# Where the merge of a hybrid decoder layer reads back the stored output of its linear attention

## The chip, the cores and the metric

The kernel runs on one core of a Trainium2 chip. Its time is the device time of one execution in microseconds (us). Five engines work side by side, each through its own instructions in order: TensorE (PE; its weight loads are listed as PEld), VectorE (DVE), ScalarE (ACT), GpSimd (POOL) and SyncE (SP), which here issues nearly all DMA transfers.

## What is computed

One layer over 1,088 tokens (1,024 of a prompt, 64 of eight samples), width 1,024. Two token mixers stand side by side: a sparse attention whose keys an indexer picks, and a gated linear attention ("GLA"). Both are projected, merged by gates, projected again, and followed by a norm, an MLP and another norm.

```python
attn = attend(q_a, k_a, v_a, q_i, k_i, z['w_i'])
...
o_b = (o_b.reshape(b, t, GLA_DV_TOT) * jax.nn.silu(z['g_b'].astype(jnp.float32))).astype(x.dtype)
branch_a = attn @ w_attn_o
branch_b = o_b @ w_gla_o
merged = jax.nn.sigmoid(z['gate_a']) * branch_a + jax.nn.sigmoid(z['gate_b']) * branch_b
return merged @ w_out, k_a, v_a, k_i, s_new.astype(x.dtype)
```

The change lies between `o_b`, `attn` and `branch_b`.

## The kernel before

**Tiling.** Activations are held feature-major: 8 pages of 128 features by 1,088 tokens, cut into token chunks of 384, 384 and 320 (`CH`, "c0", "c1", "c2" below). A product in 32-bit precision is made of three matmuls on a high and a low part of each operand (`mm3`, line 612): so each operand is split, its high part written by an ACT copy, its low part by a subtraction on DVE or POOL.

**Jobs.** `main` (line 1639) runs a list of jobs, one weight page of 128 columns each; PE's stream is made of them. Towards the end of the first phase stand the last gate jobs (PE rows `gate`), then from `merge_at` on eight jobs of branch B (`gated_job`, line 1526, PE rows `pmb`), then eight of branch A (`pma`), then the output projection (`pwo`). A job of branch B reads all eight pages of the GLA output: 24 matmuls for each of the three chunks, 72 in all. Its result is multiplied into a gate page (`mgt`) on DVE. A job's weights (`wr`) are split into `wh` (ACT) and `wl` (POOL or DVE) by `w_split`, one job ahead; `env["alone"]` makes the first job of branch B an exception, so that the second one's weights are split only after the first one's instructions.

**Other streams.** Around the jobs, generators run as streams: the prompt's softmax (`at_soft`: scores `psq`, exponentials, scaling of `pp`) and its products with the values (`at_pv`, line 1390: transposes `ppt`, split `phl`, sums `pov`), 32 units of a query tile and a head pair. Each unit ends in `tail` (line 1393): its output `ao` is split into `ahl` (two buffers, line 1402) and stored to `at_s` by two DMAs, from where branch A loads it later. The GLA output was stored to `ob_s` long before, in jobs `gb`; `ob_load` (line 1502) loads its eight pages `obl` in two pieces each (384 columns for c0, 704 for c1 and c2) and splits them into `obh` (ACT) and `obl` in place (`sub`).

**What sets the order.** All instructions are recorded in one pass by a planner: `Clock` keeps an estimated time for each engine and buffer, `Order.run` (line 297) steps the first stream of its list whose wish time is not after PE's estimated time. What is recorded first stands first in each engine's queue. `sub` (line 404) gives a subtraction to POOL when its estimate ends there before DVE's estimate plus `late`. All instructions are recorded through one line (254), so the profile shows that line throughout, and tiles tell the groups apart.

**DMA issue.** SP issues in order. By the built program each issue also waits until the eighth DMA before it has completed, so that at most eight are under way.

Of the kernel before, what the change touches and what calls it, by code (L numbers as in the profile page):

```python
# [12 lines left out]
F32 = mybir.dt.float32  # L13
F32R = mybir.dt.float32r
# [9 lines left out]
P = 128  # L24
# [30 lines left out]
LATE_I = 1.5  # L55
VAHEAD = 1
SCRATCH = 4096
OBLEAD = 3
NPV = 32
GAHEAD = 2  # L60
BLEAD = 1
DEEP = 2
# [20 lines left out]
def f32(ap):  # L83
    return ap.bitcast(F32)
# [288 lines left out]
def front(ph, tc, env, A, O):  # L373
# [13 lines left out]
    def page(name, dt=F32, shape=None):  # L387
        return clock.take(pgs.tile(shape or [P, T], dt, name=name, tag="pg", bufs=NPG), name, "pg", NPG)
# [4 lines left out]
        return clock.take(pgs.tile([p, n], dt, name=name, tag="sm", bufs=NSM), name, "sm", NSM)  # L393

    def tiny(name, n=8, dt=F32, p=P):
        return pgs.tile([p, n], dt, name=name, tag="ty", bufs=24)

    def cst(name, shape, dt=F32):
        return cs[0].tile(shape, dt, name=name, tag=name, bufs=1)

    def csg(name, shape, dt=F32):
        return gpool.tile(shape, dt, name=name, tag=name, bufs=1)

    def sub(out, a, b, late=0.0):

        n = out.free_size() if callable(out.free_size) else out.free_size
        if clock.t["pool"] + 0.0021 * n < clock.t["dve"] + 0.00104 * n + late:
            pool.tensor_tensor(out, a, b, op=OP.subtract)
        else:
            dve.tensor_sub(out, a, b)  # L410
# [897 lines left out]
    def loadq(i):  # L1308
        if i < len(units):
            qt, hp = units[i]  # L1310
            qs[i] = cs[0].tile([P, 2, P], F32R, name=f"qq{qt}{hp}", tag="qq", bufs=3)
            sp.dma_start(f32(qs[i]), f32(qa_s[2 * hp:2 * hp + 2, :, qt * P:(qt + 1) * P].rearrange("h p q -> p h q")))

    def kv_load(g):
# [75 lines left out]
    def at_pv():  # L1390
        tails = deque()

        def tail(qt, hp, po):

            yield [po]
            o = small("ao", 256)
            t = small("ao2", 256)
            act.activation(t[:64], po[64:128], AF.Copy)
            dve.tensor_tensor(o[:64], po[0:64], t[:64], op=OP.add)
            unpin(po)  # L1400
            yield [o[:64]]
            hl = cs[0].tile([P, 256], F32R, name="ahl", tag="ahl", bufs=2)
            act.activation(hl[0:64], o[:64], AF.Copy)
            sub(hl[64:128], o[:64], f32(hl[0:64]))
            yield [hl]
            c, x0 = qt // 3, (qt % 3) * P
            for e in range(2):
                sp.dma_start(view(f32(at_s[c]), 2 * hp * 64 * 768 + e * 384 + x0, [[768, 64], [64 * 768, 2], [1, P]]),
                             f32(hl[e * 64:e * 64 + 64].rearrange("p (h q) -> p h q", q=P)))

        def step():

            while tails and all(clock.ready(x) <= clock.t["pe"] + 0.3 for x in tails[0][1]):
                tails[0][1] = next(tails[0][0], None)
                if tails[0][1] is None:
                    tails.popleft()
        for _ in units:
            yield lambda: len(soft) > 0
            (qt, hp), pd = soft[0]
            vp = kv["v", hp // 2]  # L1420
            po = bank("pov", True)[:, :256]
            pend = deque()

            def flush(kt, m, hl, last):
                for j in range(m):
                    for e in range(2):
                        pe.matmul(po, vp[:, kt + j], hl[:, e, 256 * j:256 * j + 256],
                                  start=kt + j + e == 0, stop=last and j == m - 1 and e == 1)
            for kt in range(0, qt + 1, 2):
                yield pd  # L1430
                m = min(2, qt + 1 - kt)
                pt = bank("ppt")[:, :256 * m]
                for j in range(m):
                    for h in range(2):
                        pe.transpose(pt[:, (2 * j + h) * P:(2 * j + h + 1) * P], pd[h][:, (kt + j) * P:(kt + j + 1) * P], idf)
                hl = page("phl", F32R, [P, 2, 512])
                act.activation(hl[:, 0, :256 * m], pt, AF.Copy)
                dve.tensor_sub(hl[:, 1, :256 * m], pt, f32(hl[:, 0, :256 * m]))
                pend.append((kt, m, hl))
                step()  # L1440
                if len(pend) > 1:
                    yield [pend[0][2]]
                    flush(*pend.popleft(), False)
                    step()
            soft.popleft()
            while len(tails) > 1:
                yield tails[0][1]
                step()
            while pend:
                yield [pend[0][2]]  # L1450
                flush(*pend.popleft(), not pend)
            tails.append([tail(qt, hp, po), ()])
            kv["pv"] = kv.get("pv", 0) + 1
        while tails:
            yield tails[0][1]
            step()
# [42 lines left out]
    merge_at = len(jobs)  # L1499
    mark["search"] = merge_at + SEARCH  # L1500

    def ob_load():
        yield lambda: kv.get("pv", 0) >= NPV and state["job"] >= merge_at - OBLEAD or state["job"] >= merge_at
        raw = [page(f"obl{k}", F32R) for k in range(8)]
        for s in (slice(0, 384), slice(384, T)):
            for k in range(8):
                sp.dma_start(f32(raw[k][:, s]), ob_s[k][:, s])
        for c, (c0, n) in enumerate(CH):
            s = slice(c0, c0 + n)
            for k in range(8):  # L1510
                yield [f32(raw[k][:, s])]
                if c == 0:
                    ob.append((page(f"obh{k}", F32R), raw[k]))
                h, l = ob[k]
                act.activation(h[:, s], f32(l[:, s]), AF.Copy)
                sub(l[:, s], f32(l[:, s]), f32(h[:, s]))
            flags.add(("ob", c))

    gts = {}
# [147 lines left out]
    s_ts = order.add(top_sample(), slack=TS_SLACK, margin=M_TS)  # L1667
    s_main = order.add(main(), engines=())
    order.add(at_load(), at=0)
    order.add(ob_load(), slack=1.0, at=0)  # L1670
    s_pv = order.add(at_pv(), margin=M_PV, at=1)
    s_sf = order.add(at_soft(), margin=M_SF, at=2)
    env.update(ka_n=ka_n, v_n=v_n, ix_k=ix_k, ix_v=ix_v, p_b=p_b, p_q=p_q)
# [3 lines left out]
def back(ph, tc, env, A, O):  # L1677
# [9 lines left out]
    def page(name, dt=F32R):  # L1687
        return clock.take(pgs.tile([P, 2, 384], dt, name=name, tag="pg", bufs=NBP), name, "bpg", NBP)
# [7 lines left out]
        return clock.take(pgs.tile([P, 384], dt, name=name, tag="sm", bufs=NBS), name, "bsm", NBS)  # L1696

    def own(name, shape, dt=F32, bufs=1):
        return pgs.tile(shape, dt, name=name, tag=name, bufs=bufs)

    def sub(out, a, b):
        n = out.free_size() if callable(out.free_size) else out.free_size
# [89 lines left out]
    def ln(c, z, s, gi, emit, tag):  # L1792
        n = CH[c][1]
        last = z[7:] if c == 2 else []
        for k, x in enumerate([s] + last):
            yield [x]
            if k == 0:
                pm = bank("plm")
            pe.matmul(pm[:, :n], on, x, start=k == 0, stop=k == len(last))
        s2 = small("ls2")  # L1800
        off = sorted({0, P, n - P})
        yield [pm[:, :n]]
        s3 = small("ls3")
        q = None
        for f in range(9):
            if f < 8:
                dve.tensor_tensor(z[f], z[f], pm[:, :n], op=OP.subtract)
            if q is not None:
                e, x = (pool, s3) if f in (4, 6) else (dve, s2)
                e.tensor_tensor(x[:, :n], x[:, :n], q[:, :n], op=OP.add)  # L1810
            if f < 8:
                q = small("lq") if f > 1 else None
                act.activation((q if f > 1 else s3 if f else s2)[:, :n], z[f], AF.Square)
            yield ()
        dve.tensor_tensor(s2[:, :n], s2[:, :n], s3[:, :n], op=OP.add)
        yield [s2[:, :n]]
        pv = bank("plv")
        for j, o in enumerate(off):
            pe.matmul(pv[:, j:j + 1], s2[:, o:o + P], on[:, :1], start=True, stop=True)
        yield [pv[:, :3]]  # L1820
        r3 = pgs.tile([P, 4], F32, name="lr", tag="r3", bufs=2)
        act.activation(r3[:, :3], pv[:, :3], AF.Sqrt, bias=eps)
        yield [r3[:, :3]]
        dve.reciprocal(r3[:, :3], r3[:, :3])
        yield [r3[:, :3]]
        r = bank("plr", True)
        for j, o in enumerate(off):
            pe.matmul(r[:, o:o + P], r3[:, j:j + 1].to_broadcast([P, P]), idf, start=True, stop=True)
        yield [r[:, :n]]
        run = []  # L1830
        for f in range(10):
            if f < 8:
                dve.scalar_tensor_tensor(z[f], z[f], lnp[:, gi, f:f + 1], r[:, :n], op0=OP.mult, op1=OP.mult)
                run.append(emit(f, z[f], lnp[:, gi + 1, f:f + 1]))
            for e in run:
                next(e, None)
            yield ()
        unpin(r)
        normed.add((tag, c))
# [544 lines left out]
```

## Time and profile before

| | us |
|---|---|
| median of 3 runs (2121.95 to 2124.35) | 2122.55 |
| profiled execution, its own time | 2120.89 |
| its span | 2119.2 |
| PE busy | 2052.5 (97%) |
| idle of PE between 930 and 960, by the table of stretches | 17.84 |

The page gives busy times of each engine, then the span in 40 slices, the DMA queues, the chain of work that ended last, and the costliest groups. PE is busy nearly all the time, so the page's list of groups says little of what an edit is worth; the table of stretches and the chain in order of time show the few places where PE stands still. Times of rows are us from the start of the span. A matmul's row gives its duration with the pipeline's fill in it; the pitch from one row's start to the next is what it adds to a stream. A row's last bracket names the idle time before it and what ended it.

### The profile page before, as it was taken

The page shows a single profiled execution, that of the slowest core. Times are in us where ns is not written, and L with a number is a line of the kernel's source. Part 1 is how long each engine was busy: PE and PEld are TensorE (multiplying, and loading weights), DVE is VectorE, ACT ScalarE, POOL GpSimd, SP SyncE. Part 2 cuts the span into 40 slices and gives each one's busy share as a digit, 9 for nine tenths or more (in the row PEclk, how much of TensorE's full clock was granted, in tenths as well). Part 3 has the DMA queues.
Part 4 walks back from the last instruction along what each step waited for, and adds up shares of the span by engine and source line. Part 5 has one row for each costly group of instructions (what it writes and reads, how often), then busy time and mean ns, then how long its engine had stood idle before and what let it go on. Part 6 is the DMA issues. An engine that isn't in the chain of part 4 may idle for free.

```text
span 2119.2 us, 34591 instructions
## 1 busy us (share of the span) xinstructions
PE 2052.5 (97%) x12507; PEld 1958.7 (92%) x12507; DVE 1316.4 (62%) x2775; ACT 1024.7 (48%) x2008; POOL 776.2 (37%) x576
## 2 busy tenths in 40 slices
PE   7899999999999999978999999999999999999997
PEld 7888998998989999978998899989999999999996
DVE  7786997778765675743166845555654445466635
ACT  5566236565656755663023424445453333345543
POOL 4244220303141113215134336645655443354452
PEclk9999999999999999998999999999999999999998
DMA  7564411212123224244483234544523442135542
GB/s 263 228 182 112 147 37 33 82 47 88 37 88 124 79 84 133 88 152 146 177 283 108 72 90 119 180 124 137 158 87 110 142 131 81 65 131 163 185 149 81
DMA packets 182859, 260.78 MB, mean 123 GB/s; under 512 B 21392, under 2 KB 118672, under 8 KB 182688
## 3 DMA queue, kind: packets, MB, share of 16 engines
q1 hardware_dynamic: 175136, 233.14, 33.6%
q0 software_dynamic: 7552, 25.43, 3.8%
q8 instruction: 98, 1.61, 0.3%
q14 instruction: 73, 0.60, 0.1%
HBM read 209.00 MB, written 49.51 MB: 122 GB/s over the span
## 4 chain that ended last, share of the span: by engine, by line
PE 88%; DVE 3%; issue 3%; DMA 3%; POOL 1%; ACT 1%; SPq 0%; ACTq 0%; DVEq 0%; POOLq 0%
PE pf L254 33%; PE gate L254 9%; PE psv L254 5%; PE gb L254 5%; PE pwo L254 4%; PE pmb L254 4%; PE psc L254 3%; PE po L254 3%; PE qb L254 2%; PE kb L254 2%; PE qa L254 2%; PE pma L254 2%; PE qi L254 2%; PE psq L254 2%; PE pov L254 1%
## 5 line engine op out<-in xcount | busy, mean ns | idle before, releaser
L254 PE MATMUL pf<-a,w 128*128 128x384 f32 (+1 forms) x2304 | 400.0, 329 | 2.3 <-POOL a L254 1.3
L254 PE MATMUL pf<-h,w 128*128 128x384 f32 (+1 forms) x2304 | 396.6, 329 | 3.0 <-POOL w L254 1.8
L254 PEld LDWEIGHTS pf<-h,w 128*128 128x128 f32 x2304 | 380.2, 189 | 5.4 <-POOL w L254 2.1
L254 PEld LDWEIGHTS pf<-a,w 128*128 128x128 f32 x2304 | 378.8, 188 | 5.5 <-POOL a L254 1.8
L254 POOL TENSOR_TENSOR wl<-wr,wh 128x1024 fp32r<-128x1024 f32 (+1 forms) x67 | 155.1, 2317 | 519.4 <-ACT wh L254 417.4
L254 POOL TENSOR_TENSOR w<-wr,w 128x512 fp32r<-128x512 f32 x131 | 187.3, 1437 | 134.9 <-ACT w L254 121.9
L254 ACT ACTIVATE w<-wr 128x512 fp32r<-128x512 f32 x272 | 156.7, 618 | 55.4 <-PE pf L254 24.9
L254 DVE TENSOR_TENSOR w<-wr,w 128x512 fp32r<-128x512 f32 x141 | 147.1, 1052 | 54.8 <-ACT w L254 50.7
L254 POOL TENSOR_TENSOR a<-fr,a 128x384 fp32r<-128x384 f32 (+1 forms) x58 | 56.9, 980 | 202.0 <-ACT a L254 202.0
L254 PE MATMUL gate<-xh,wh 128*128 128x384 f32 (+1 forms) x384 | 130.7, 340 | 0.0
L254 DVE TENSOR_TENSOR acc<-acc,pf 128x384 f32<-128x384 f32 (+1 forms) x136 | 72.8, 538 | 85.5 <-PE pf L254 85.2
L254 PE MATMUL gate<-xh,wl 128*128 128x384 f32 (+1 forms) x384 | 125.6, 327 | 0.0
L254 PE MATMUL gate<-xl,wh 128*128 128x384 f32 (+1 forms) x384 | 125.5, 327 | 0.0
L254 ACT ACTIVATE wh<-wr 128x1024 fp32r<-128x1024 f32 (+1 forms) x75 | 74.6, 1006 | 79.7 <-DMA wr<-wgo 42.4
L254 DVE TENSOR_TENSOR fr<-fr,pf 128x384 f32<-128x384 f32 (+1 forms) x96 | 50.8, 529 | 89.5 <-ACT fr L254 89.1
L254 ACT ACTIVATE fr<-pf 128x384 f32<-128x384 f32 (+1 forms) x96 | 44.9, 468 | 120.0 <-PE pf L254 118.9
L254 DVE TENSOR_SCALAR_CACHE_REDUCE jk<-sc,gb_f 128x896 int8<-128x896 f32 (+2 forms) x96 | 92.7, 966 | 1.0
L254 ACT ACTIVATE a<-fr 128x384 fp32r<-128x384 f32 (+1 forms) x96 | 48.7, 508 | 84.2 <-DVE fr L254 84.2
L254 DVE TENSOR_SCALAR_CACHE_REDUCE jk<-sc,ga_f 128x1024 int8<-128x1024 f32 (+2 forms) x96 | 88.4, 921 | 1.1
L254 PE MATMUL psv<-wh,xh 128*128 128x256 f32 (+1 forms) x288 | 83.9, 291 | 0.0
L254 PE MATMUL psv<-wh,xl 128*128 128x256 f32 (+1 forms) x288 | 81.2, 282 | 0.0
L254 PE MATMUL psv<-wl,xh 128*128 128x256 f32 (+1 forms) x288 | 81.2, 282 | 0.0
(460 smaller groups left out, 5109.5 us busy)
## 6 DMA issues: line engine op xcount, KB each, us to landing
wr<-wff SPq DMA_DIRECT2D x256, 256.0 KB, 2.9
wr<-w SPq DMA_DIRECT2D x43, 512.0 KB, 4.6
ckr<-kT SPq DMA_DIRECT2D x256, 64.0 KB, 2.0
ga_s<-gate SPq DMA_DIRECT2D x16, 544.0 KB, 3.1
ci_s<-cig SPq DMA_DIRECT2D x16, 512.0 KB, 6.7
kir<-ci_s SPq DMA_DIRECT2D x16, 512.0 KB, 6.6
wr<-wout SPq DMA_DIRECT2D x13, 512.0 KB, 5.8
mgp<-ga_s SPq DMA_DIRECT2D x16, 384.0 KB, 6.9
```

The costliest lines, as they stand in the source:

```text
L254: r = f(*a, **k)
```

## The change

`ob_load` is cut in two. The new `ob_load` only loads, may begin one job before the merge (`OBLEAD = 1`; it no longer asks that all 32 units of `at_pv` are recorded), and asks at each load that, of three in flight (`OBFLY`), the oldest has landed by the planner's estimate. It takes no engine's time into account (`engines=()`). A stream of its own, `ob_split`, splits a piece once its load is recorded, and stands third in the list, behind the loads and the value products. Its subtractions get `late=OBLATE`, which is -9.0. The stored outputs `ahl` get four buffers (`NAHL`) for two. Everything else in the diff hands further tiles to the planner's accounts (`clock.take`) and leaves the order of all instructions outside the stretch shown below as it was; which buffer a page takes differs.

```diff
-OBLEAD = 3
-NPV = 32
+OBLEAD = 1
+OBFLY = 3
+NAHL = 4
+OBLATE = -9.0
...
-            hl = cs[0].tile([P, 256], F32R, name="ahl", tag="ahl", bufs=2)
+            hl = clock.take(cs[0].tile([P, 256], F32R, name="ahl", tag="ahl", bufs=NAHL), "ahl", "ahl", NAHL)
...
+    obr, gone = [], []
+
     def ob_load():
-        yield lambda: kv.get("pv", 0) >= NPV and state["job"] >= merge_at - OBLEAD or state["job"] >= merge_at
-        raw = [page(f"obl{k}", F32R) for k in range(8)]
-        for s in (slice(0, 384), slice(384, T)):
+        yield lambda: state["job"] >= merge_at - OBLEAD
+        fly = deque()
+        for j, s in enumerate((slice(0, 384), slice(384, T))):
             for k in range(8):
-                sp.dma_start(f32(raw[k][:, s]), ob_s[k][:, s])
+                if j == 0:
+                    obr.append(page(f"obl{k}", F32R))
+                if len(fly) >= OBFLY:
+                    yield [fly.popleft()]
+                sp.dma_start(f32(obr[k][:, s]), ob_s[k][:, s])
+                fly.append(f32(obr[k][:, s]))
+                gone.append((k, s))
+
+    def ob_split():
         for c, (c0, n) in enumerate(CH):
             s = slice(c0, c0 + n)
             for k in range(8):
-                yield [f32(raw[k][:, s])]
+                yield lambda: any(i == k and o.start <= s.start and s.stop <= o.stop for i, o in gone)
+                yield [f32(obr[k][:, s])]
                 if c == 0:
-                    ob.append((page(f"obh{k}", F32R), raw[k]))
+                    ob.append((page(f"obh{k}", F32R), obr[k]))
                 h, l = ob[k]
                 act.activation(h[:, s], f32(l[:, s]), AF.Copy)
-                sub(l[:, s], f32(l[:, s]), f32(h[:, s]))
+                sub(l[:, s], f32(l[:, s]), f32(h[:, s]), late=OBLATE)
             flags.add(("ob", c))
...
-    order.add(ob_load(), slack=1.0, at=0)
+    order.add(ob_load(), engines=(), at=0)
+    order.add(ob_split(), slack=1.0, at=2)
```

SP's queue before, from the weights of branch B's second job on (`wr`; `qq` are queries for the last score tiles, `ga_s` a stored gate):

```order
L254 DMA wr_0_9916<-wgo 128x1024
L254 DMA at_s_84<-ahl 64x2x128 x2
L254 DMA qq_10010<-qa_s 128x2x128
L254 DMA at_s_84<-ahl 64x2x128 x2
L254 DMA qq_10060<-qa_s 128x2x128
L254 DMA at_s_84<-ahl 64x2x128 x2
L254 DMA ga_s_93<-gate_9922 128x1088
L254 DMA mgt<-ga_s_86 128x1088
...
L254 DMA obl_10204<-ob_s_82 128x704
L254 DMA at_s_83<-ahl 64x2x128 x12
```

Now, from the same weights on:

```order
L256 DMA wr_0_9916<-wgo 128x1024
L256 DMA obl_9930<-ob_s_75 128x384
...
L256 DMA obl_9932<-ob_s_76 128x704
L256 DMA at_s_84<-ahl 64x2x128 x2
L256 DMA obl_9934<-ob_s_77 128x704
L256 DMA obl_9936<-ob_s_78 128x704
L256 DMA obl_10061<-ob_s_79 128x704
L256 DMA ga_s_93<-gate_9922 128x1088
L256 DMA mgt<-ga_s_86 128x1088
L256 DMA mgt<-ga_s_87 128x1088
L256 DMA at_s_83<-ahl 64x2x128 x2
L256 DMA obl_10063<-ob_s_80 128x704
```

Before, all 16 loads stood between the gate pages and the last twelve stores; now 13 stand between the stores and queries ahead of the last gate's store, and three behind it.

ACT's queue before, from the last chunk of the last gate on:

```order
L254 ACTIVATE gate_9922<-gate_2_10113 128x320
L254 ACTIVATE ao_10233<-pov 64x256
L254 ACTIVATE phl<-ppt 128x512
L254 ACTIVATE pp,mx<-pp,mx 128x128
L254 ACTIVATE pp<-pp,rc 128x128
L254 ACTIVATE pp,mx<-pp,mx 128x128
L254 ACTIVATE ahl<-ao 64x256
L254 ACTIVATE pp<-pp,rc 128x128
L254 ACTIVATE ao_10266<-pov 64x256
L254 ACTIVATE phl<-ppt 128x256
L254 ACTIVATE ahl<-ao 64x256
```

Now, in the same place:

```order
L256 ACTIVATE obh_10212<-obl_9930 128x384
L256 ACTIVATE gate_9922<-gate_2_10129 128x320
L256 ACTIVATE pp<-pp,rc 128x128
L256 ACTIVATE ao_10233<-pov 64x256
L256 ACTIVATE phl<-ppt 128x512
L256 ACTIVATE pp,mx<-pp,mx 128x128
L256 ACTIVATE pp<-pp,rc 128x128
L256 ACTIVATE pp,mx<-pp,mx 128x128
L256 ACTIVATE ahl<-ao 64x256
L256 ACTIVATE obh_10263<-obl_9932 128x384
L256 ACTIVATE pp<-pp,rc 128x128
L256 ACTIVATE ao_10272<-pov 64x256
```

Two splits of the GLA output now stand among the last softmax steps, and one scaling of `pp`, which DVE did, stands on ACT. The other 22 follow among the last `ahl`, `ao` and `phl`, where all 24 stood behind all but the last two `ahl`.

POOL's queue before, from the low weights of branch B's first job to those of its second:

```order
L254 TENSOR_TENSOR wl_0_9919<-wr_0_9625,wh_0_9918 128x1024
L254 TENSOR_TENSOR ahl<-ao,ahl 64x256 x4
L254 TENSOR_TENSOR obl_10197<-obl_10197,obh_10307 128x384
L254 TENSOR_TENSOR ahl<-ao,ahl 64x256
...
L254 TENSOR_TENSOR obl_10203<-obl_10203,obh_10336 128x320
L254 TENSOR_TENSOR wl_0_10460<-wr_0_9916,wh_0_10459 128x1024
```

Now:

```order
L256 TENSOR_TENSOR wl_0_9919<-wr_0_9625,wh_0_9918 128x1024
L256 TENSOR_TENSOR ahl<-ao,ahl 64x256 x7
L256 TENSOR_TENSOR wl_0_10460<-wr_0_9916,wh_0_10459 128x1024
```

POOL's eleven subtractions of `obl` are gone: all 24 stand on DVE. PE's order is the same but for one pair of `pov`, which moves behind the first 18 matmuls of branch B.

## Rows read from the trace of the kernel before

**Rows 1.** The table of stretches, 930 to 970: from and to, length, busy time of PE, PEld, DVE, ACT, POOL (instructions), TensorE's granted clock as a share of its full one, DMA share, GB/s.

```profile
930.00:940.00 10.00, 8.89 (x67) 8.62 (x66) 6.09 (x29) 7.74 (x24) 1.47 (x2) 1.00 0.08 22
940.00:950.00 10.00, 2.74 (x10) 1.67 (x10) 2.03 (x7) 2.58 (x10) 0.72 (x1) 0.66 1.03 373
950.00:960.00 10.00, 0.53 (x2) 0.32 (x2) 1.35 (x4) 2.16 (x6) 0.72 (x1) 0.50 0.75 272
960.00:970.00 10.00, 9.55 (x37) 9.12 (x37) 9.59 (x11) 9.71 (x26) 9.31 (x9) 0.64 0.26 59
```

**Rows 2.** The chain of work that ended last, in order of time, 940 to 1062: start, length, what.

```profile
941.30 5.03 DMA obl<-ob_s
...
951.33 5.73 DMA at_s<-ahl
...
957.17 0.42 ACT ahl L254
...
975.53 2.59 POOL wl L254
...
978.17 82.94 PE pmb L254 x502
```

**Rows 3.** SP's instructions in order of time, 920 to 950: start, length, what, count.

```profile
920.12 0.38 SPq L254 DMA_DIRECT2D wr<-wgo  x1
...
927.50 0.38 SPq L254 DMA_DIRECT2D qq<-qa_s  x1
...
939.01 0.34 SPq L254 DMA_DIRECT2D ga_s<-gate  x1
...
940.77 9.02 SPq L254 DMA_DIRECT2D obl<-ob_s  x16
950.39 17.45 SPq L254 DMA_DIRECT2D at_s<-ahl  x12
```

**Rows 4.** ACT's instructions in order of time, 938 to 971.

```profile
938.58 0.41 ACT L254 ACTIVATE gate<-gate 128x320 f32<-128x320 f32 x1
...
941.92 0.40 ACT L254 ACTIVATE pp<-pp,rc 128x128 f32<-128x128 f32 x1
...
942.74 0.39 ACT L254 ACTIVATE phl<-ppt 128x256 fp32r<-128x256 f32 x1
957.17 0.42 ACT L254 ACTIVATE ahl<-ao 64x256 fp32r<-64x256 f32 x1 [14.04 <-DMA at_s<-ahl]
...
964.77 5.88 ACT L254 ACTIVATE obh<-obl 128x384 fp32r<-128x384 f32 x15
970.55 1.04 ACT L254 ACTIVATE wh<-wr 128x1024 fp32r<-128x1024 f32 x1
```

**Rows 5.** PE's matmuls in order of time, 936 to 977.

```profile
936.27 0.56 PE L254 MATMUL psq<-kar,qq 128*128 128x128 f32 x4
...
943.18 1.04 PE L254 MATMUL pov<-phl,vpr 128*128 128x256 f32 x2 [1.49 <-ACT phl L254]
944.01 0.63 PE L254 MATMUL ppt<-idf,pp 128*128 128x128 f32 x2
...
960.35 0.63 PE L254 MATMUL pmb<-obh,wh 128*128 128x384 f32 x1
...
966.71 0.52 PE L254 MATMUL pmb<-obh,wl 128*128 128x384 f32 x1
967.03 0.40 PE L254 MATMUL pmb<-obh,wh 128*128 128x384 f32 x1
...
971.78 0.33 PE L254 MATMUL pmb<-obh,wh 128*128 128x384 f32 x1
971.96 0.33 PE L254 MATMUL pmb<-obl,wh 128*128 128x384 f32 x1
...
976.42 0.34 PE L254 MATMUL pmb<-obh,wh 128*128 128x384 f32 x1
```

**Rows 6.** The groups of DVE, different shapes apart: what, count, busy us, mean ns of one, idle before.

```profile
L254 DVE TENSOR_TENSOR a<-fr,a 128x384 fp32r<-128x384 f32 x22 | 12.3, 558 | 13.0 <-ACT a L254 13.0
L254 DVE TENSOR_TENSOR obl<-obl,obh 128x384 fp32r<-128x384 f32 x9 | 10.2, 1186 | 0.4 <-ACT obh L254 0.4
L254 DVE TENSOR_TENSOR xl<-xr,xh 128x384 fp32r<-128x384 f32 x16 | 9.7, 674 | 3.1 <-ACT xh L254 3.1
...
L254 DVE TENSOR_TENSOR a<-fr,a 128x320 fp32r<-128x320 f32 x16 | 8.1, 509 | 8.6 <-ACT a L254 8.6
...
L254 DVE TENSOR_TENSOR obl<-obl,obh 128x320 fp32r<-128x320 f32 x4 | 4.0, 1047 | 0.0
```

**Rows 7.** DMA issues of the whole span: what, queue, count, KB each, median us from issue to landing.

```profile
mgt<-ga_s SPq DMA_DIRECT2D x8, 544.0 KB, 5.2
...
qq<-qa_s SPq DMA_DIRECT2D x32, 128.0 KB, 2.4
at_s<-ahl SPq DMA_DIRECT2D x64, 64.0 KB, 2.3
...
obl<-ob_s SPq DMA_DIRECT2D x8, 352.0 KB, 5.7
...
obl<-ob_s SPq DMA_DIRECT2D x8, 192.0 KB, 5.0
```

More of the change, by code (lines that the diff above doesn't have):

```diff
@@ L395, in tiny @@
     def tiny(name, n=8, dt=F32, p=P):
-        return pgs.tile([p, n], dt, name=name, tag="ty", bufs=24)
+        return clock.take(pgs.tile([p, n], dt, name=name, tag="ty", bufs=24), name, "ty", 24)
     def cst(name, shape, dt=F32):
-        return cs[0].tile(shape, dt, name=name, tag=name, bufs=1)
+        return clock.take(cs[0].tile(shape, dt, name=name, tag=name, bufs=1), name, "cst " + name, 1)
     def csg(name, shape, dt=F32):
-        return gpool.tile(shape, dt, name=name, tag=name, bufs=1)
+        return clock.take(gpool.tile(shape, dt, name=name, tag=name, bufs=1), name, "csg " + name, 1)
     def sub(out, a, b, late=0.0):
@@ L1310, in loadq @@
             qt, hp = units[i]
-            qs[i] = cs[0].tile([P, 2, P], F32R, name=f"qq{qt}{hp}", tag="qq", bufs=3)
+            qs[i] = clock.take(cs[0].tile([P, 2, P], F32R, name=f"qq{qt}{hp}", tag="qq", bufs=3), f"qq{qt}{hp}", "qq", 3)
             sp.dma_start(f32(qs[i]), f32(qa_s[2 * hp:2 * hp + 2, :, qt * P:(qt + 1) * P].rearrange("h p q -> p h q")))
@@ L1698, in own @@
     def own(name, shape, dt=F32, bufs=1):
-        return pgs.tile(shape, dt, name=name, tag=name, bufs=bufs)
+        return clock.take(pgs.tile(shape, dt, name=name, tag=name, bufs=bufs), name, "own " + name, bufs)
     def sub(out, a, b):
@@ L1820, in ln @@
         yield [pv[:, :3]]
-        r3 = pgs.tile([P, 4], F32, name="lr", tag="r3", bufs=2)
+        r3 = clock.take(pgs.tile([P, 4], F32, name="lr", tag="r3", bufs=2), "lr", "r3", 2)
         act.activation(r3[:, :3], pv[:, :3], AF.Sqrt, bias=eps)
```

## The prediction

> **What bounds the kernel now.** The page first: PE is busy 97% of the span, so an edit gains only where PE stands still or runs at a lower clock. The table of stretches shows the widest such place: between 930 and 960 PE is idle for 17.84 us of 30, and the granted clock is 1.00, 0.66, 0.50 and 0.64 in the four stretches to 970 [rows 1]; of TensorE's two levels, 2.4 and 1.2 GHz, it is at the lower one from about 943 on, after some 4 us of sparse work. Then the chain in order of time, which names the reason: loads `obl` from 941.30, the store `at_s` behind them to 957.06, ACT's `ahl`, and only then work again; POOL's `wl` to 978.12 is the last wait, and from 978.17 PE runs `pmb` for 82.94 us without one [rows 2]. Then SP: the 16 loads are issued from 940.77 to 949.79, and the twelve stores of the last six `ahl` stand behind them [rows 3]. ACT shows the price: an `ahl` waited 14.04 us for a store to free one of two buffers, from 943.13 to 957.17, with all splits of the GLA output queued behind it [rows 4]. So PE did not wait for the loads as such, but for a small store behind 4.46 MB (8 x (192 + 352) KB) [rows 7]: at 373 GB/s [rows 1] that is 12.0 us.
>
> **Loads moved forward, and the stores in front of the last three.** 13 loads go out before the last gate's store, from 920.50 on, where `wr` ends, instead of 940.77 [rows 3]. An issue costs 9.02 / 16 = 0.56 us with its gap. What they delay: three of them stand ahead of the next store and query, so SP is about 1.7 us later there. The query issued at 927.50 [rows 3] is read by `psq` at 936.27 [rows 5]; a query's median landing is 2.4 us [rows 7], so it has 6.4 us to spare; I take nothing for it. Behind the loads in the queue wait stores and queries, and for those ACT and PE; with the median of 5.0 to 5.7 us to land [rows 7] and DMA nearly unused between 930 and 940 (share 0.08 [rows 1]), the 13 are in by 942. The last three follow the gate's store (939.01 [rows 3], 0.42 later for the split now ahead of it), two gate pages and two `ahl` stores, thus at some 942 to 943.5; in flight with them are 3 x 544 KB of gates. 1.67 + 0.13 + 1.08 MB at 373 GB/s are 7.7 us from 939.5: landed by about 948. ACT needs them at 952 (below). The first `ahl` store of the new buffers' second round is needed back at 952 too, is issued near 941.4, and lands with the gates by about 947. So with four buffers I cost this wait at nothing; its cover is these 4 to 5 us, and if it goes, the rival "the store's wait moves" below is its price.
>
> **The tail gets longer.** The last softmax steps are a serial chain over ACT, DVE and PE. Into it the change puts two `obh` on ACT (5.88 us for 15, so 0.42 each for 384 columns and 0.37 for 320 [rows 4]), one scaling of 0.40 that DVE did [rows 4], and two subtractions on DVE of 0.56 [rows 6]: 0.84 + 0.40 + 1.12, and 0.15 of hand-overs, 2.5 us. The `phl` of 942.74 [rows 4] then comes at 945.25. Its consumer `pov` starts 0.44 after it, as 943.18 stands to 942.74; `pov` and the next `ppt` took 943.18 to 944.64, 1.46 us [rows 5]; DVE's half of `phl` is within that. So branch B begins at about 947.1 instead of 960.35 [rows 5]: **13.25 us**.
>
> **Branch B's first job.** It took from 960.35 to 976.42, 16.07 us [rows 5]. A matmul of 384 columns adds 0.32 at the lower level (966.71 to 967.03) and 0.175 at the upper (971.78 to 971.96) [rows 5]; the level rose 6.7 us after PE's steady work began. I let that recur: in 6.7 us, 0.5 of them for the moved pair of `pov`, PE does 19 of c0's 24 matmuls, the last five take 0.9; c1 24 x 0.175 = 4.2; c2 24 x 0.146 (0.175 x 320/384) = 3.5. Sum 15.3, so it ends at 962.4: **0.8 us**.
>
> Does the feed keep up? DVE has 22 subtractions left, 14 x 0.56 + 8 x 0.51 [rows 6], and beside them four `ao` and two `phl` of 0.42 and one gate product, 0.55: 15.0 us, less what one of these waits for PE. It begins the first at 946.1, and stands still some 1.1 us at the product for c0, which needs PE's last matmul of c0 at 954.7 and is queued ahead of the last two c1 subtractions. That gives about 962 by the plain sum; several rows overlap by 0.07 at both ends, so 960 to 962, and PE reaches the last one's matmuls at 962. Just in time; I charge nothing and keep 1 us for the range.
>
> Why one engine may cost no more than two: before, 13 subtractions on DVE took 1186 and 1047 ns and 11 stood on POOL; subtractions of the same shapes without POOL's take 674, 558 and 509 ns [rows 6]. I take 0.56 because `a<-fr,a` has the same place between an ACT copy and PE; 0.67 would add 0.11 x 22 = 2.4 us to DVE. The Trainium skill ("SBUF — State Buffer", section "Who interferes with whom") says that a VectorE operation with two SBUF inputs and a GpSimd operation that reads SBUF exclude each other, the second waiting for the first one's end; by that rule nothing is lost by taking POOL out, and by the opposite reading, that 1186 ns is the price of the subtraction itself, the sum would be that of the rival "DVE binds". The doubled rows agree with the rule.
>
> **Second job's weights.** Their split is recorded behind the first job. ACT's 24 `obh` and what stands between end near 958.7 (from the last of c0 at 949.2: 8 x 0.42 + 8 x 0.37 + three `ahl` and two `ao` of 0.4, and 1.2 for waits on DVE's `ao`); `wh` 1.04 [rows 4], then `wl` 2.59 [rows 2], which finds POOL free: 962.3. The third matmul of the job needs it at 962.4 + 0.35 = 962.75: no wait. Before, 976.42 to 978.17 was 1.75 us for two matmuls and the wait, now 0.35: **1.4 us**.
>
> **Nothing else moves.** From there on PE has no wait for 82.94 us [rows 2], and the order, the loads and the stores of the later stages hang on these matmuls, so the gain is kept. Sum: 13.25 + 0.8 + 1.4 = 15.45 us off the profiled execution's 2120.89, 2105.4. That execution lies 1.66 below the median of the runs, 2122.55; against the median the forecast is 2122.55 - 15.45, **2107**.
>
> **Its own range.** If the level does not fall in the shorter gap, `wl` becomes last, at 961.2 at the earliest with ACT unhindered, and the gain is 978.17 - 961.2 = 17: 2105.5. With 0.67 for a subtraction, 1 us more in the tail and 1 us in the feed: 2110. A microsecond for the spread of medians on the low side: 2104 to 2110.
>
> **The rivals.**
> *The low level lasts through the whole first job* (DVE's feed breaks PE's work up): 5 + 24 matmuls of 384 at 0.145 more and 24 of 320 at 0.12 more, 7.1 us: 2114. For it: DVE is nearly the bound; against: the level rose before in the same situation, with both engines feeding.
> *The change does not bring the last loads earlier:* the three behind the gate land as late as before, at 957.06 less the 0.6 of a store, say 956.5 instead of 948; then ACT, which needs them at 952, is 4.5 late, and so is `wl`: 2111. For it: they are issued at 942, no earlier than the same pieces before (to 949.79) by more than 7; against: the 13 others are out of the way.
> *The store's wait moves:* `ahl` stops again for 14.04 us, now at 952, for a buffer whose store stands behind gates and loads: 2107 + 14 = 2121, no change. Against: the queue holds 1.8 MB then, not 4.46 and gates. The Trainium skill ("DMA: Bandwidth & Descriptors", section "Queues, rings and completion order") says that each DMA engine consumes a ring's descriptors in ring order; by that the store waits for what was issued before it, which the row of 951.33, ended at 957.06, agrees with.
> *DVE binds:* if 1186 and 1047 ns are the subtraction's own, 22 of them take 25.0 us, and with 3.1 for the others DVE ends at 946.7 + 28.1 = 974.8; the third matmul of the second job follows at 975.6 instead of 978.17: 2120, no change. Against: the rows without POOL.
> *Slower:* PE stays at the lower level beyond the first job, place `pmb`, price 0.145 us a matmul. From 15.45 / 0.145 = 107 further matmuls on the gain is gone, from 136 on (with 4.2 us) it is slower by over 0.2%. Through the first three jobs it is 7.1 + 96 x 0.145 + 48 x 0.12 = 26.8 us: 2134. Against: before, 18 matmuls at the lower level were enough.
>
> **How the numbers follow.** Forecast 0.72, low level through the first job 0.08, last loads late 0.08, the store's wait moves 0.04, DVE binds 0.04, slower 0.04. The forecast and the late loads hold 0.80, so 2104 to 2113. A difference under 0.2%, 4.2 us, can hardly be told from none here; beyond it lie the first three cases: faster 0.88, same 0.08, slower 0.04.
>
> **What would show it.** After: no wait of ACT `ahl` for `at_s`; the first `pmb` near 947 (step one), its clock up by 954, the first job's end near 962 and no wait for `wl` over 0.5 us; DVE's `obl` near 0.56 us; the last three loads landed before 950. A first `pmb` after 952 or an `ahl` waiting over 3 us would prove the sum wrong in its first term, `obl` rows near 1.1 us in the feed, a clock below 1 after 960 in the second.

## The result and the profile after

| | before | changed |
|---|---|---|
| median of five executions (us) | 2122.55 (2121.54 to 2125.21) | 2111.73 (2107.75 to 2115.03) |
| ratio, 95% interval | | 0.9945 [0.9927, 0.9964] |
| profiled execution, its span | 2119.2 | 2106.1 |
| median of all executions of this study | 2122.75 (42) | 2108.89 (17) |

The changed kernel is faster: the interval of the ratio lies below 1. The first five executions say 10.8 us, all 17 of the unaltered changed kernel 13.9, the two profiled ones 13.1; the forecast was 15.45.

The table of stretches of the changed kernel, columns as in [rows 1]:

```profile
930.00:940.00 10.00, 9.57 (x72) 9.29 (x70) 5.80 (x28) 7.67 (x24) 1.46 (x2) 1.00 0.77 259
940.00:950.00 10.00, 4.74 (x17) 4.11 (x18) 6.85 (x20) 7.97 (x23) 1.58 (x2) 0.69 0.89 311
950.00:960.00 10.00, 10.00 (x60) 10.00 (x60) 9.90 (x22) 9.05 (x23) 4.81 (x3) 0.97 0.15 38
960.00:970.00 10.00, 8.44 (x50) 8.12 (x49) 1.71 (x4) 2.22 (x3) 6.19 (x4) 1.00 0.66 209
```

Between 930 and 960 PE is idle for 5.69 us where it was idle for 17.84, and between 930 and 940 DMA is busy (share 0.77) where it was nearly unused (0.08). SP's queue shows the 13 loads, then the gate's store, then the last three:

```profile
920.80 0.38 SPq L256 DMA_DIRECT2D wr<-wgo  x1
921.28 1.83 SPq L256 DMA_DIRECT2D obl<-ob_s  x3
...
926.70 1.06 SPq L256 DMA_DIRECT2D obl<-ob_s  x2
...
928.60 2.36 SPq L256 DMA_DIRECT2D obl<-ob_s  x5
...
935.37 1.55 SPq L256 DMA_DIRECT2D obl<-ob_s  x3
940.10 0.32 SPq L256 DMA_DIRECT2D ga_s<-gate  x1
...
943.16 1.57 SPq L256 DMA_DIRECT2D obl<-ob_s  x3
944.82 16.59 SPq L256 DMA_DIRECT2D at_s<-ahl  x10
```

ACT waits for no DMA in this stretch. Its longest wait at an `ahl` is 0.55 us, for DVE, against 14.04 for a store in [rows 4]:

```profile
946.11 0.38 ACT L256 ACTIVATE phl<-ppt 128x256 fp32r<-128x256 f32 x1
...
956.56 0.42 ACT L256 ACTIVATE ahl<-ao 64x256 fp32r<-64x256 f32 x1 [0.55 <-DVE ao L256]
956.88 2.26 ACT L256 ACTIVATE obh<-obl 128x320 fp32r<-128x320 f32 x6
959.05 1.04 ACT L256 ACTIVATE wh<-wr 128x1024 fp32r<-128x1024 f32 x1
```

PE's matmuls, as in [rows 5]: the first `pmb`, the change from 0.32 to 0.18 us a matmul, and the second job's first and third:

```profile
947.66 0.67 PE L256 MATMUL pmb<-obh,wh 128*128 128x384 f32 x1
...
950.37 0.46 PE L256 MATMUL pmb<-obh,wl 128*128 128x384 f32 x1
950.67 0.34 PE L256 MATMUL pmb<-obh,wh 128*128 128x384 f32 x1
...
961.22 0.34 PE L256 MATMUL pmb<-obh,wh 128*128 128x384 f32 x1
...
963.30 0.44 PE L256 MATMUL pmb<-obh,wl 128*128 128x384 f32 x1 [1.56 <-POOL wl L256]
```

What PE waited for there stands in POOL's instructions in order of time:

```profile
953.85 1.00 POOL L256 TENSOR_TENSOR ahl<-ao,ahl 64x256 fp32r<-64x256 f32 x1 [2.21 <-ACT ahl L256]
957.06 3.75 POOL L256 TENSOR_TENSOR ahl<-ao,ahl 64x256 fp32r<-64x256 f32 x1 [2.21 <-ACT ahl L256]
960.89 2.36 POOL L256 TENSOR_TENSOR wl<-wr,wh 128x1024 fp32r<-128x1024 f32 x1
```

Beside them DVE, in order of time:

```profile
956.45 3.76 DVE L256 TENSOR_TENSOR obl<-obl,obh 128x384 fp32r<-128x384 f32 x9
```

POOL's last `ahl` took 3.75 us while DVE ran nine subtractions in a row (one of 384 columns and eight of 320; the row names the first); only then came `wl`.

**A yardstick within the stretch.** Executions reach this place at different times (SP issues the second job's weights `wr` between 919.61 and 929.68 in the profiles of this study), so the runs are compared by a *distance*: from that issue to the start of PE's unbroken work. Where PE still has a break or the lower level behind it, the distance is reckoned back from the output projection: its longest piece in the chain starts 120.80 us after unbroken work begins (978.17 to 1098.97 before, 963.30 to 1084.10 changed). Before it is 978.17 - 920.12 = 58.05 [rows 2, 3], changed 963.30 - 920.80 = 42.50: the stretch gained **15.55 us**.

Of that the span kept 13.1. Here are that piece of the output projection (`pwo`) and the first piece of the MLP (`pf`) in the chain of the kernel before:

```profile
1098.97 29.08 PE pwo L254 x166
...
1175.06 6.16 PE pf L254 x25
```

And those of the changed kernel:

```profile
1084.10 29.08 PE pwo L256 x166
...
1161.96 6.17 PE pf L256 x25
```

The way between them is 76.09 us before and 77.86 now: 1.77 lost. In it PE stands still for `mg`, equally long in both:

```profile
1131.17 3.35 PE L254 MATMUL pwo<-mg,w 128*128 128x384 f32 x9 [2.94 <-DVE mg L254]
```

```profile
1116.28 0.79 PE L256 MATMUL pwo<-mg,w 128*128 128x384 f32 x3 [2.94 <-DVE mg L256]
```

The table of stretches shows the lower level behind that. The kernel before:

```profile
1131.00:1133.00 2.00, 1.83 (x6) 1.78 (x6) 2.00 (x3) 2.00 (x5) 1.73 (x2) 0.50 0.98 377
1133.00:1135.00 2.00, 1.77 (x6) 1.07 (x5) 2.00 (x3) 0.79 (x2) 2.00 (x2) 0.65 0.81 304
1135.00:1137.00 2.00, 1.24 (x7) 0.92 (x7) 2.00 (x3) 0.00 (x0) 0.82 (x1) 1.00 0.05 20
```

The changed one:

```profile
1118.00:1120.00 2.00, 1.76 (x5) 1.25 (x6) 2.00 (x2) 0.50 (x1) 2.00 (x2) 0.50 0.18 68
1120.00:1122.00 2.00, 1.78 (x6) 1.27 (x5) 2.00 (x4) 0.00 (x0) 0.48 (x1) 0.50 0.00 0
1122.00:1124.00 2.00, 2.00 (x8) 2.00 (x8) 1.97 (x4) 0.00 (x0) 0.00 (x0) 0.50 0.00 0
1124.00:1126.00 2.00, 2.00 (x11) 2.00 (x11) 0.59 (x2) 0.00 (x0) 0.00 (x0) 0.82 0.00 0
```

Before, the lower level lasted some 3.4 us, and PE waited for `mg` behind it anyway; now some 6.8, the last of them on full work. The rest: the changed execution came 0.68 us later to the stretch (920.80 for 920.12). 15.55 - 1.77 - 0.68 = 13.1, the difference of the spans; from the MLP on both take 944.14 us.

### The profile page after: what moved, and what is told of

Its sections match the earlier page's. It is cut to its first block, busy times and chain, and to the rows that moved or that the text cites. A ratio compares the mean times of both kernels' runs of the same rounds, so it can differ in the third digit from the quotient of the medians.

```text
span 2106.1 us, 34590 instructions
## 1 busy us (share of the span) xinstructions
PE 2053.3 (97%) x12507; PEld 1960.0 (93%) x12507; DVE 1320.5 (63%) x2784; ACT 1025.2 (49%) x2009; POOL 764.5 (36%) x566
## 4 chain that ended last, share of the span: by engine, by line
PE 87%; DVE 5%; issue 4%; ACT 2%; DMA 1%; POOL 1%; SPq 0%; ACTq 0%; DVEq 0%; POOLq 0%
PE pf L256 33%; PE gate L256 9%; PE psv L256 5%; PE gb L256 5%; PE pwo L256 4%; PE pmb L256 4%; PE psc L256 3%; PE po L256 3%; PE qb L256 2%; PE kb L256 2%; PE qa L256 2%; PE pma L256 2%; PE psq L256 2%; PE pov L256 1%; PE pob L256 1%
```

## The experiments

All are compared with the kernel before on the same chip; its medians were 2122.31 (17 executions, beside x1 to x4), 2123.95 (9, x5 to x8) and 2121.29 (11, x9 to x11).

| run | median (us) | ratio to before, 95% | distance | gain of the distance |
|---|---|---|---|---|
| x1, changed again | 2108.42 | 0.9924 [0.9904, 0.9944] | 42.50 | 15.55 |
| x2, before, four buffers | 2119.13 | 0.9981 [0.9969, 0.9993] | 54.07 | 3.98 |
| x3, changed, two buffers | 2107.79 | 0.9919 [0.9902, 0.9937] | 42.52 | 15.53 |
| x4, changed, POOL shares | 2107.69 | 0.9919 [0.9900, 0.9937] | 43.57 | 14.48 |
| x5, loads late, interleaved | 2115.68 | 0.9958 [0.9944, 0.9972] | 50.88 | 7.17 |
| x6, loads early, one block | 2109.36 | 0.9926 [0.9913, 0.9940] | 44.96 | 13.09 |
| x7, low weights on DVE | 2105.99 | 0.9910 [0.9896, 0.9923] | 41.25 | 16.80 |
| x8, splits before softmax | 2110.13 | 0.9936 [0.9922, 0.9950] | (other order) | |
| x9, changed again | 2108.29 | 0.9932 [0.9911, 0.9953] | 42.53 | 15.52 |
| x10, as x7 | 2104.04 | 0.9912 [0.9892, 0.9933] | 41.16 | 16.89 |
| x11, before, earlier trigger | 2110.40 | 0.9941 [0.9922, 0.9960] | 47.50 | 10.55 |

**x1 and x9: the changed kernel again.**

> The changed kernel once more, unaltered, for a second profile and as the yardstick of the runs beside it. Its five executions ran from 2107.75 to 2115.03 us, those of before only from 2121.54 to 2125.21. Theory one (clock): the stretch of the change is the same in each execution (unbroken work of PE from 963.3 +- 0.5), and what differs is how long TensorE stays at its lower level after stalls elsewhere, as at 1118 to 1125 in the first profile; then a slower execution shows lower granted clocks in stretches outside 920 to 1000. Theory two (loads): the stretch itself varies, by when the last loads land; then the unbroken work starts up to 7 us later in a slower execution.

> The changed kernel again, unaltered, on the same chip as the version with the low weights on DVE, for a direct comparison: 2107 to 2112, distance from the issue of the second job's weights to unbroken work 42.5.

In all three profiles of the unaltered changed kernel the distance is 42.5. What varies lies outside: the way from projection to MLP was 77.86, 78.38 and 78.23 us (in x1 with some 10 us of the lower level, by the table of stretches), and `wr` was issued at 920.80, 921.49 and 921.32. In these three the stretch does not vary, as theory one has it; but their spans (2106.1 to 2107.4) are too alike to show what the slowest executions, at 2115, lose. Two profiles of other versions were of long executions: x2's took 2128.88 us, with a median of 2119.13, and x6's 2116.37, with 2109.36. They issue `wr` at 929.68 and 926.63, and their granted clock in the first 100 us is 0.91, where the other profiles of this study have 0.93 to 0.98. So what these two lost lies mostly ahead of the stretch, which is again theory one.

**x2: four buffers alone, in the kernel before.**

```diff
-            hl = cs[0].tile([P, 256], F32R, name="ahl", tag="ahl", bufs=2)
+            hl = cs[0].tile([P, 256], F32R, name="ahl", tag="ahl", bufs=4)
```

> The kernel before with four buffers for the stored outputs and nothing else changed. In the kernel before unbroken work of PE started at 978.17, in the changed one at 963.30, 14.87 earlier. Theory one (the store behind the loads was the wait, as the prediction has it): ACT passes 943.13 without the 14.04 us, the first pmb comes at 947 to 948, the splits follow the loads, which land until 953 to 954, on both engines as before (18 us for 24), and the unbroken work starts at 966 to 968: 10 to 12 of the 14.87 us from this edit alone, 2110 to 2113. Theory two (the loads themselves must come earlier): the first pmb stays later than 953 and less than 7 us are won, 2116 or more.

```profile
954.20 0.42 ACT L254 ACTIVATE ahl<-ao 64x256 fp32r<-64x256 f32 x1 [0.55 <-DVE ao L254]
...
955.34 1.04 ACT L254 ACTIVATE obh<-obl 128x384 fp32r<-128x384 f32 x2
966.68 0.42 ACT L254 ACTIVATE ahl<-ao 64x256 fp32r<-64x256 f32 x1 [10.31 <-DMA at_s<-ahl]
967.00 1.33 ACT L254 ACTIVATE obh<-obl 128x384 fp32r<-128x384 f32 x3
```

ACT passes the old place, splits two pieces, and stops two outputs later, for 10.31 us, for a store that still stands behind the 16 loads. The first `pmb` does come 13.95 us earlier after `wr` (955.96 - 929.68 = 26.28 for 40.23), but the splits stand behind the waiting `ahl`. The number expected under theory one is missed (3.98 us of distance and some 3 us of median for 10 to 12), and the time is the one that theory two gave, though the late first `pmb` of theory two did not come: more buffers move the wait by two outputs and do not end it, since the stores of the last six outputs all stand behind the loads. SP's queue and the chain of x2 show how the store hung on the loads:

```profile
950.33 9.00 SPq L254 DMA_DIRECT2D obl<-ob_s  x16
```

```profile
956.91 5.69 DMA obl<-ob_s
962.67 4.27 DMA at_s<-ahl
```

A DMA row of the chain runs from issue to landing. The load of 956.91 is not the last: all 16 were issued by 959.33. It is the eighth DMA before the store of 962.67, so its landing let SP issue that store. The store then took 4.27 us, for a median of 2.3 [rows 7], with later loads still under way: the last one, issued at 959.01, took 7.2 us, to 966.2. The store that ended ACT's wait of 10.31 us stands two before it: issued at 960.86, it took 5.7 us, to 966.6. So these stores waited for loads twice, for their turn to be issued and again until they landed. The Trainium skill ("DMA: Bandwidth & Descriptors", section "Queues, rings and completion order") has each DMA engine take its ring's descriptors in ring order; the trace agrees, both stores having landed behind the last load, by 0.4 and 0.8 us.

**x3: two buffers in the changed kernel.**

```diff
-NAHL = 4
+NAHL = 2
```

> The changed kernel with two buffers for the stored outputs instead of four; the order of all instructions stays. Theory one (the queue was the cause, the buffers only cover it): with 13 loads out of the way a store lands within some 3 to 4 us, so an output of ACT waits at most 2 us, and the unbroken work starts at 963.3 to 965.5; 0 to 2 us slower than the changed kernel. Theory two (the buffers are needed): the wait comes back behind the gate pages and the last three loads, more than 5 us at about 946 to 950, and the unbroken work starts after 968.

Distance 42.52, and no `ahl` waited over 0.56 us. With the loads out of the way the two added buffers are worth nothing here.

**x4: POOL shares the subtractions again.**

```diff
-OBLATE = -9.0
+OBLATE = 0.0
```

> The changed kernel with the splits' subtractions shared between DVE and POOL again, as the planner's estimates decide (9 of the remaining ones on POOL). Theory one (DVE and POOL hold each other up while both read two tiles, as the prediction took it): DVE's subtractions of 384 columns go from 0.54 us towards the 1.19 of before, POOL's stay far above 1 us, the last split ends 2 to 5 us later than 960.2, and the unbroken work starts at 965 to 968. Theory two (two engines do more than one): the splits end earlier than 960.2, the wait of 1.56 us for the second job's low weights shrinks, and the unbroken work starts before 963.

Groups of `obl`, shapes apart, as in [rows 6], in the changed kernel:

```profile
L256 DVE TENSOR_TENSOR obl<-obl,obh 128x384 fp32r<-128x384 f32 x16 | 9.7, 638 | 2.3 <-ACT obh L256 2.1
L256 DVE TENSOR_TENSOR obl<-obl,obh 128x320 fp32r<-128x320 f32 x8 | 3.3, 476 | 0.0
```

The same groups of x4, on DVE and on POOL:

```profile
L256 DVE TENSOR_TENSOR obl<-obl,obh 128x384 fp32r<-128x384 f32 x10 | 9.4, 967 | 2.5 <-ACT obh L256 2.5
L256 DVE TENSOR_TENSOR obl<-obl,obh 128x320 fp32r<-128x320 f32 x5 | 4.8, 972 | 0.1
L256 POOL TENSOR_TENSOR obl<-obl,obh 128x384 fp32r<-128x384 f32 x6 | 7.2, 1216 | 2.6 <-ACT obh L256 2.3
```

Fifteen subtractions on DVE beside nine on POOL keep DVE busy for 14.2 us, all 24 alone for 13.0. POOL's help costs DVE more than it takes over, and the distance grows by 1.07. That is theory one in its direction and its longer rows (0.64 to 0.97 us and 0.48 to 0.97), with a smaller price than the 1.7 us and more (965 for 963.3) that it gave; the medians don't show it (2107.69, beside 2108.42 for x1). The Trainium skill ("SBUF — State Buffer", section "Who interferes with whom") calls the contention of these two engines an exclusive lock on a shared pair of ports; the rows agree.

**x5: loads interleaved with the stores, but not earlier.**

```diff
-OBLEAD = 1
+OBLEAD = 0
```

> The changed kernel with the loads begun at the merge and not one job earlier: three of them stand behind the gate pages, the other 13 between and behind the stores, three in flight. Distance from SP's issue of the second job's weights to the start of unbroken PE work: 58.05 us before, 42.50 changed, 54.07 with four buffers alone. Theory one (what counts is that no store stands behind many loads): ACT waits for no store; only the loads come later, the pieces of 704 columns behind the last output's store, so the splits end some 6 to 8 us later: 48 to 51. Theory two (what counts is that the loads are early): little is left of the gain, above 54.

Distance 50.88, as theory one has it, but for one `ahl` that waits 0.92 us for a store. Eleven waits of ACT for `obl` pieces, 0.35 to 1.97 us each, take 7.5 us in its place, the longest being

```profile
958.29 0.52 ACT L256 ACTIVATE obh<-obl 128x384 fp32r<-128x384 f32 x1 [1.97 <-DMA obl<-ob_s]
```

So by this order of steps 7.2 of the 15.55 us come with the stores no longer behind all the loads, 8.4 more with the loads being early. Early loads free the stores too (x11), so the shares overlap.

**x6: all 16 loads early, in one block ahead of three outputs' stores and two queries.**

```diff
-OBFLY = 3
+OBFLY = 16
```

> The changed kernel with all 16 loads issued in one block at the last gate, ahead of three outputs' stores and two queries. Theory one (early is enough, as DMA is nearly unused there): stores and queries issue about 9 us later but nothing needs them before 936, the last splits' data is there sooner, and the distance is 41.5 to 43.5. Theory two (the block moves the wait, as four buffers did): scores `psq` or an output of ACT wait for what stands behind the block, by over 3 us, and the distance is above 45.

Unbroken work starts 43.54 after `wr`, just over the range of theory one; with 1.4 us more at the lower level behind it the distance is 44.96, between the two theories. No wait of ACT for a store is seen. The edit costs 2.5 us, but not through the stores alone: the splits come earlier in ACT's queue too, ten of them ahead of the last softmax step, for two, and PE waits 1.17 and 1.86 us for the second job's `wh` and `wl`, where the changed kernel waits 1.56.

**x7 and x10: the second job's low weights on DVE.**

```diff
-    def w_split(i):
+    def w_split(i, late=None):
...
-            sub(l, r, f32(h), WLATE if 1 < state["job"] < mix_at - 1 else 0.0)
+            sub(l, r, f32(h), (WLATE if 1 < state["job"] < mix_at - 1 else 0.0) if late is None else late)
...
             flags.add(("ob", c))
+        w_split(state["split"], -99.0)
+        state["split"] += 1
```

> The changed kernel with the second job's weights split right behind the last piece of the GLA output, the low part on DVE instead of POOL. In the changed kernel POOL's last `ahl` took 3.75 us (0.73 to 1.00 for the others), from 957.06 to 960.81, while DVE ran nine subtractions in a row until 960.20; `wl` started at 960.89 and PE waited 1.56 us for it. Theory one (POOL is held up as long as DVE reads two tiles): DVE does `wl` from 960.2 to about 961.4, PE waits at most 0.3 us, and the distance shrinks from 42.50 to 40.8 to 41.3; POOL's `ahl` then ends even later, 961.5 or more, since DVE has one more such operation. Theory two (the 3.75 us have another reason, on POOL): the wait is gone as well, but POOL's `ahl` ends no later than before, 960.8.

> The version with the second job's low weights on DVE again, beside the changed kernel. If its gain in the first run (distance 41.25 for 42.50) is its own, it is 1.2 us faster here too, within the spread of executions that the clock makes (some 3 us); if it is noise, the distance is 42.5.

PE has no wait at the second job in either run, and the distance is 41.25 and 41.16. POOL's `ahl` in x7, in order of time:

```profile
958.58 3.75 POOL L256 TENSOR_TENSOR ahl<-ao,ahl 64x256 fp32r<-64x256 f32 x1 [2.21 <-ACT ahl L256]
```

And DVE beside it:

```profile
957.97 3.75 DVE L256 TENSOR_TENSOR obl<-obl,obh 128x384 fp32r<-128x384 f32 x9
961.66 1.75 DVE L256 TENSOR_TENSOR wl<-wr,wh 128x1024 fp32r<-128x1024 f32 x1
```

`ahl` ends 40.02 us after `wr` (962.33 - 922.31), as in the changed kernel (960.81 - 920.80 = 40.01): not later: on this point the number is theory two's, though DVE has one more such operation behind. Yet it ends 0.6 us after the ninth subtraction both times, about its own 0.73. So by these rows it got its turn behind the nine; why it got none between them, they don't say. The three `ahl` before it in the changed kernel, beside five, four and three subtractions, took 0.86, 0.87 and 1.00 us.

Beside each other x10 has 2104.04 and x9 2108.29: this is the fastest version of the study, by 1.2 to 1.4 us in distance. The rest of the 4 us lies outside the stretch. In the two profiles with the edit the way from projection to MLP takes 77.44 and 77.23 us and the time from there on 942.5, where the three of the changed kernel have 77.86 to 78.38 and 944.1 to 944.3; whether the edit does that is not shown.

**x8: the splits ahead of the softmax.**

```diff
-OBLEAD = 1
+OBLEAD = 2
...
-    order.add(ob_split(), slack=1.0, at=2)
...
     s_sf = order.add(at_soft(), margin=M_SF, at=2)
+    order.add(ob_split(), slack=3.0, at=2)
```

(The section on the change calls the splits' stream third in the list; once all streams are added it stands behind the softmax stream too, and this diff lifts it over that one.)

> The changed kernel with the loads begun two jobs ahead and the splits' stream put ahead of the softmax stream, with 3.0 us of slack: most splits stand among the last two gates, branch B's first job follows the last gate at once, and the last softmax steps and value products stand among the matmuls of its first jobs. In the changed kernel PE was idle for 5.26 us between 940 and 950, at the lower level from about 942 to 950.5, and waited 1.56 us for `wl`. Theory one (PE's idle time at the tail is only an order): PE runs through from the gates to branch B, 6 to 8.5 us less than the changed kernel, 2100 to 2103. Theory two (ACT and DVE are the bound there): the splits hold up the softmax steps and the gates behind them, PE gets new gaps of the same size in the gates or the first jobs, and the time is that of the changed kernel within 3 us.

Theory two. The first `pmb` follows the last gate at once, at 930.68, but between 920 and 980 PE is idle for 2.91 + 2.26 + 0.65 + 3.03 = 8.85 us, for 0.43 + 5.26 + 1.56 = 7.25 in the changed kernel. ACT's splits waited for PE's gates and then for a load, with the softmax steps behind them in its queue:

```profile
926.96 0.52 ACT L256 ACTIVATE obh<-obl 128x384 fp32r<-128x384 f32 x1 [7.27 <-PE gate L256]
936.23 0.52 ACT L256 ACTIVATE obh<-obl 128x384 fp32r<-128x384 f32 x1 [3.29 <-DMA obl<-ob_s]
```

The softmax steps that were put off then ran in short pieces among branch B's jobs, the last `ahl` at 989.45.

**x11: one line of the kernel before.**

```diff
-        yield lambda: kv.get("pv", 0) >= NPV and state["job"] >= merge_at - OBLEAD or state["job"] >= merge_at
+        yield lambda: state["job"] >= merge_at - 1
```

> The kernel before with one line changed: its loads are issued, all 16 in one block, as soon as the last gate job begins, without asking that all value products are recorded. Two buffers, POOL sharing the subtractions and one stream for loads and splits stay; the splits thus stand among the last gate and the last softmax steps. Theory one (the early issue carries the whole gain): ACT waits for no store by more than 1 us, and the distance is 42 to 46 for 58.05 before. Theory two (the other parts are needed): with the splits ahead of the softmax steps, stores behind the block and two buffers, the waits come back elsewhere, and it is above 50.

An earlier trigger alone brings 10.55 of the 15.55 us, with two buffers and POOL sharing. The waits of ACT for stores are 0.56 and 0.78 us. Unbroken work starts at a distance of 44.80, within theory one; with the lower level behind it, as in the table, it is 47.50, between the two theories, and the whole gain is not there. What is lost lies at the second job's weights, whose split stands behind the last two `ahl`, and in the lower level after these waits (17 matmuls at 0.32 us):

```profile
963.85 0.44 PE L254 MATMUL pmb<-obh,wh 128*128 128x384 f32 x1 [1.87 <-ACT wh L254]
...
966.34 0.69 PE L254 MATMUL pmb<-obh,wl 128*128 128x384 f32 x1 [1.87 <-POOL wl L254]
```

## Why the prediction came out as it did

The forecast, 15.45 us in the stretch, met 15.55 there. That it met it so closely is luck in two of its terms, as its own steps show, with the 0.68 us of later arrival taken out:

- **Start of branch B, 13.25.** Measured 40.23 - (947.66 - 920.80) = 13.37. The tail's `phl` came at 945.43 (946.11 less 0.68) for 945.25. Right, and for the reason given: x2, where the wait moved with the buffers, and x5, where the stores no longer stand behind all the loads, show that the store behind the loads was the wait. They and x11 add what the prediction did not separate: stores freed but loads late win 7.17 of the 15.55 us, loads early and nothing else 10.55. The last three loads were to land by 948; in x3, with the same order of loads, the last was issued at 945.65 and took 5.5 us, which is 949.8 in the changed kernel's time, late but within the cover.
- **The buffers.** They were costed at nothing with the store's four to five us of cover. x3 shows that two do as well, so this part of the edit bought nothing.
- **First job, 0.8.** Measured 16.07 - (961.22 - 947.66) = 2.51. Mis-sized: the level was taken to rise 6.7 us after PE's steady work began, as before; it rose 2.9 us after the first `pmb`, at about 950.5. DVE's feed did not bind: subtractions of 0.64 and 0.48 us, the last one ended at 960.2, and PE stood still for none. 1186 ns was the price beside POOL (967 in x4, where POOL shares again), so the rival "DVE binds" is out.
- **No wait for `wl`, 1.4.** Measured 1.75 - 2.08 = -0.33. The step "which finds POOL free" failed, and with it the sign "no wait for `wl` over 0.5 us", which was 1.56: POOL was in an `ahl` until 960.81, 0.7 us after `wh` was there. `wl` itself ended at 962.57 after the 0.68, forecast 962.3. So the chain of splits, `wh` and `wl`, set the end, not PE: what PE won in the first job it lost in this wait. Two errors of 1.7 us cancel; what was right is the end of `wl`, which came out 0.3 us late. x7, which takes `wl` off POOL, wins 1.25 of the 1.56 us of that wait.
- **The gain is kept.** It fell short by 1.77 us in the profile, between projection and MLP. That is TensorE's level after a stall of equal length. Whether the change brings it about is open: the way took 76.09 us in the one profile of before, 77.11 in x2, which has the same order, and 77.86 to 78.38 in the three of the changed kernel; but its altered versions range from 76.02 (x8) to 77.98 (x6). The profile that the forecast started from may have been a short one at this place; but the medians of 42 and 17 executions, too, differ by 13.9 us and not by 15.55. What decides how long the level stays down is open as well.

Of the rivals, the low level through the whole first job, the late loads and the moved wait did not come; the last is what x2 shows where the loads stay. Of the medians 2111.73 lies 1.7 above the forecast's own range (2104 to 2110) and within the wider one (2104 to 2113); the later 2108.42 and 2108.29 lie within both.

## What to carry to other kernels

When an engine waits for a small store, look at what stands ahead of it in the issuing queue: here two more buffers only moved the wait two outputs on, while issuing large loads earlier, where the DMA was idle, ended it. A subtraction that takes twice its usual time beside another engine's is no reason to share the work: find its time alone, and count operations of the other engine, however small, that will stand behind it. A sum is best checked between two events of the same stretch, since arrival times and clock levels elsewhere move the total by more than a microsecond.

## What was not expected of the hardware

A POOL subtraction of 0.73 us took 3.75 beside nine subtractions of DVE in a row, much alike in all six profiles with this order on both engines (3.70 to 3.76, in the changed kernel, x1, x3, x7, x9 and x10), and ended some 0.6 us after the ninth. The same stall of PE, 2.94 us long, was followed by some 3.4 us at the lower level in the profile of before, 6.8 in the first of the changed kernel and 10 in x1, which is the same kernel. Sixteen loads in one block, 9 us of SP's queue, in front of stores and queries (x6) cost only 2.5 us, with the splits' order changed as well.
